# VectorE in program order through an attention stage, with the output bank emptied by ScalarE

## The chip, the core and the metric

The kernel runs on one core of one Trainium2 chip. The metric is the device time of one execution in microseconds. TensorE (PE in the profile) multiplies matrices and writes to the accumulation banks, VectorE (DVE) and ScalarE (ACT) read those banks, GpSimd (POOL) works on the on-chip memory alone, and SyncE (SP) issues the transfers.

## The reference

One layer of a hybrid encoder on 1024 frames of width 1024. Three mixers work on the same normalized input: latent attention (MLA, 8 heads), forgetting attention (FoX, 8 heads) and a state-space scan (SSM). Their outputs are merged with sigmoid gates, and a gated MLP follows. Cut to what matters here, it computes for each of the 16 attention heads, in blocks of 128 query rows:

```python
s = einsum('qd,kd->qk', q_blk, k) * scale          # scores of 128 rows
p = softmax(bias_mask(i, s), axis=-1)               # keys up to the row's own block
out = einsum('qk,kd->qd', p, v)
...
xBC = silu(causal_dwconv(xBC, conv_w, conv_b))      # depthwise convolution of the SSM input, 4 taps
g = sigmoid(u_gate + b_gate)                        # gates of the three mixers
```

## The kernel before

All matrices are float32. To keep the precision, each operand is split into a high and a low part, and a product is made of two or three passes over the parts.

**Stages.** Normalization and the projections come first, then the attention stage (about 435 to 980 us in the profile), the state-space stage (to about 1205 us), the merge of the branches, the output projection and the MLP. The change touches the attention stage, lines 870 to 1026.

**The fill.** Two projections have no hurry: the input of the convolution (12 blocks of 128 channels) and the gates (24 blocks). The generator `all_fill` (L777) makes them in 36 blocks of 48 matmuls of 128x512 (L794), and hands back control after every six, which it counts as 1.3 us. These matmuls fill TensorE wherever the attention and the state-space stage would leave it idle. Behind each convolution block `conv_done` (L748) sets a chain of later work: a scaling on GpSimd (L766), six multiply-adds on VectorE, the taps (L759), two tanh on ScalarE (L772), two products on VectorE (L763) and a store.

**How the order is made.** A model clock `clk` runs over the stage in the emitting program. `merge` (L821) takes pieces of several generators in turn, by the share of their planned time that is done, and advances the clock by each piece's planned cost. `later(us, fn)` (L704) puts an instruction into a queue with a due time; `run_until` emits those that are due. So there are two orders: the order in which the program emits, made of due times, and the order in which each engine gets its instructions. Under `tc.manual_schedule(engines={PE})` (L999) TensorE gets them as they are emitted. For the other engines a scheduler places them by its own simulation of the kernel.

**A row of scores** (`score_row`, L870). Row block i has i + 1 key blocks, in one chunk or, from the fifth on, in two. For each chunk two or three matmuls go into one of three banks `s` (L884), the mask is added by one more (L887), and VectorE takes the negative maximum (L889, due 0.1 us after the matmuls). With two chunks VectorE takes the smaller of both (L896, due at 0.8). ScalarE takes the exponential of each chunk (L899, due at 0.9), which frees the bank, and VectorE and GpSimd normalize the row (L904 to L906, due at 2.6).

**A unit of values** (`values`, L917). A unit is a pair of row blocks. The probabilities are transposed by TensorE into one of two banks `tp` (L952), ScalarE copies them as the high half (L957), VectorE subtracts for the low half (L958, due at 0.6), and the value matmuls (L924 to L932) add up in one half of the bank `o`, two pairs of key blocks later. Units take the two halves of this one bank in turn. At the unit's end `done` (L934) empties it: ScalarE copies partitions 64 to 127 (L937, due at 0.5), and VectorE adds partitions 0 to 63 to that copy (L940, due at 0.9); the result is stored to `att_d` (L941).

**The start and the end.** Ahead of the first head `merge([], 8.0)` (L1001) runs six pieces of fill alone. In the state-space stage the fill goes on with the shares of FILL_SSD (L986), until it is used up near the end of that stage; the last chunk's transposes (L1169) follow the norm at L1156 and L1161.

Of the kernel before, what the change touches and what calls it, by code (L numbers as in the profile page):

```python
# [11 lines left out]
F32 = mybir.dt.float32  # L12
# [3 lines left out]
AF = mybir.ActivationFunctionType  # L16
ALU = mybir.AluOpType
# [25 lines left out]
def block_kernel(ctx: ExitStack, tc: tile.TileContext, x, positions, norm_mix_g, w_in, b_gate,  # L43
# [5 lines left out]
    V, A, G, T, SY = nc.vector, nc.scalar, nc.gpsimd, nc.tensor, nc.sync  # L49
# [85 lines left out]
    def uid(s):  # L135
        cnt[0] += 1
        return f"{s}_{cnt[0]}"
# [566 lines left out]
    def later(us, fn):  # L704
        h = [clk[0] + us, uid(""), fn]
        queue.append(h)
        return h
# [106 lines left out]
    def advance(gen):  # L814
        c = next(gen, None)
        if c is not None:
            clk[0] += c
            run_until(clk[0])
        return c

    def merge(streams, fill_us):  # L821

        st = [[e[0], max(e[1], 0.01), 0.0, e[2] if len(e) > 2 else 0.0] for e in streams]
        owed[0] += fill_us
        if owed[0] > 0.65:
            st.append([fill, owed[0], 0.0, 0.0])
        while st:
            s_ = min(st, key=lambda e: e[3] + (1.0 - e[3]) * e[2] / e[1])
            if s_[0] is fill and s_[2] >= s_[1] - 0.65:
                owed[0] -= s_[2]  # L830
                st.remove(s_)
                continue
            c = advance(s_[0])
            if c is None:
                st.remove(s_)
            else:
                s_[2] += c
# [32 lines left out]
    def score_row(o, i, pn):  # L870
        mask = (mmla, mfox)[o.br]
        n = i + 1
        chunks = row_chunks(i)
        p_, _ = a_pm.get()
        nmx, _ = a_nmx.get()
        rs, rl = a_rs.get()
        pss = []
        qs = slice(i * P, i * P + P)
        for ci, (a, b) in enumerate(chunks):
            ps, pl = a_s.get()  # L880
            w = max(b - a, 256)
            last = ci == len(chunks) - 1
            for i_, (q_, k_) in enumerate(o.passes):
                T.matmul(ps[:, :w], q_[:, qs], k_[:, a:a + w], start=i_ == 0,  # L884
                         stop=not last and i_ == len(o.passes) - 1)
            if last:
                T.matmul(ps[:, b - a - P:b - a], identb, mask, start=False, stop=True)  # L887
            c = len(o.passes) * w / 2400
            later(c + 0.1, lambda ps=ps, ci=ci, a=a, b=b: V.reduce_max(  # L889
                nmx[:, ci:ci + 1], ps[:, :b - a], axis=AX, negate=True))  # L890
            pss.append((ps, pl))
            if not last:
                yield c
        two = len(chunks) == 2
        if two:
            later(c + 0.8, lambda: V.tensor_tensor(nmx[:, 2:3], nmx[:, 0:1], nmx[:, 1:2], op=ALU.min))  # L896
        nb = nmx[:, 2:3] if two else nmx[:, 0:1]
        for ci, (a, b) in enumerate(chunks):
            pss[ci][1][0] = later(c + 0.9 + 0.1 * ci, lambda ci=ci, a=a, b=b: A.activation(  # L899
                p_[:, a:b], pss[ci][0][:, :b - a], AF.Exp, bias=nb, accum_out=rs[:, ci:ci + 1]))  # L900

        def norm():
            if two:
                V.tensor_add(rs[:, 2:3], rs[:, 0:1], rs[:, 1:2])  # L904
            V.reciprocal(rs[:, 3:4], rs[:, 2:3] if two else rs[:, 0:1])  # L905
            G.tensor_scalar(p_[:, 0:n * P], p_[:, 0:n * P], rs[:, 3:4], 0.0, op0=ALU.mult, op1=ALU.add)  # L906

        rl[0] = later(c + 2.6, norm)
        pn.append((p_, rl))
        yield c + 0.05  # L910
# [6 lines left out]
    def values(o, jp, pn):  # L917

        po = o_acc[:, jp % 2, :]

        def pv(kp, th, tl):
            full = kp < jp
            k0, k1 = 2 * kp, 2 * kp + 1
            T.matmul(po, o.vv[:, k0, :], th[:, 0:256], start=kp == 0, stop=False)  # L924
            if full:
                T.matmul(po, o.vv[:, k1, :], th[:, 256:512], start=False, stop=False)
                T.matmul(po, o.vv[:, k1, :], tl[:, 256:512], start=False, stop=False)
            else:
                T.matmul(po[0:64, 128:256], o.vv[:, k1, 0:64], th[:, 256:384], start=False, stop=False)
                T.matmul(po[0:64, 128:256], o.vv[:, k1, 64:128], th[:, 256:384], start=False, stop=False)  # L930
                T.matmul(po[0:64, 128:256], o.vv[:, k1, 0:64], tl[:, 256:384], start=False, stop=False)
            T.matmul(po, o.vv[:, k0, :], tl[:, 0:256], start=False, stop=not full)  # L932

        def done():  # L934
            o1, l1 = a_o1.get()
            o2, l2 = a_o2.get()
            later(0.5, lambda: A.activation(o1, po[64:128, :], AF.Copy))  # L937

            def fin():
                V.tensor_add(o2, po[0:64, :], o1)  # L940
                SY.dma_start(att_d[o.br][o.h * 64:o.h * 64 + 64, jp * 256:jp * 256 + 256], o2)  # L941

            l1[0] = l2[0] = o_last[jp % 2] = later(0.9, fin)

        for _, rl in pn:
            force(rl[0])
        for kp in range(jp + 1):
            pt, pl = a_tp.get()
            off = 0
            for k in (2 * kp, 2 * kp + 1):  # L950
                for qi in ((0, 1) if k <= 2 * jp else (1,)):
                    T.transpose(pt[:, off:off + P], pn[qi][0][:, k * P:k * P + P], ident)  # L952
                    off += P
            th, _ = a_th.get()
            tl, _ = a_tl.get()
            c = 0.11 * off / P
            later(c + 0.05, lambda th=th, pt=pt, off=off: A.activation(th[:, :off], pt[:, :off], AF.Copy))  # L957
            pl[0] = later(c + 0.6, lambda th=th, tl=tl, pt=pt, off=off: V.tensor_sub(  # L958
                tl[:, :off], pt[:, :off], f32(th[:, :off])))
            pend.append((pv, kp, th, tl, pl, jp, done if kp == jp else None))  # L960
            yield c
            if len(pend) > PVLAG:
                run_pv()
                yield 0.44
# [3 lines left out]
    o_last = [None, None]  # L968
# [18 lines left out]
    with ExitStack() as pt__:  # L987
        atp = pt__.enter_context(TP("atp", 2))
        psp = pt__.enter_context(TP("psa", 1, space=PSUM))
        atp_lead = atp.tile([P, 64], F32, name="lead4", tag="lead4", bufs=1)  # L990
        a_pm = Ring(atp, [P, S], F32, "pm", 6)
        a_nmx, a_rs = (Ring(atp, [P, 4], F32, n, 4) for n in ("nmx", "rs"))
        a_th, a_tl = (Ring(atp, [P, 512], F32R, n, PVLAG + 2) for n in ("pth", "ptl"))
        a_o1 = Ring(atp, [64, 256], F32, "o1", 1)
        a_o2 = Ring(atp, [64, 256], F32, "o2", 2)
        a_s = Ring(psp, [P, 512], F32, "s", 3)
        a_tp = Ring(psp, [P, 512], F32, "tp", 2)
        o_acc = psp.tile([P, 2, 256], F32, name="o", tag="o")
        with tc.manual_schedule(engines={mybir.EngineType.PE}):  # L999
            names = [(br, h) for br in range(2) for h in range(8)]  # L1000
            merge([], 8.0)  # L1001
            units = [(n, jp) for n in range(16) for jp in range(4)]
            heads = {0: load_head(atp, *names[0])}
            load_values(atp, heads[0])
            done = []
            for n in range(len(units) + 2):
                st, share = [], 0.0
                if n < len(units):
                    hn_, jp = units[n]
                    if jp == 0 and hn_ + 1 < 16:  # L1010
                        heads[hn_ + 1] = load_head(atp, *names[hn_ + 1])
                    if jp == 3 and hn_ + 1 < 16:
                        load_values(atp, heads[hn_ + 1])
                    pn = []
                    done.append((heads[hn_], jp, pn))
                    share += cost_s(jp)
                    st.append((scores(heads[hn_], jp, pn), cost_s(jp, len(heads[hn_].passes))))
                if n >= 2:
                    share += cost_v(done[n - 2][1])
                    st.append((values(*done[n - 2]), cost_v(done[n - 2][1])))  # L1020
                merge(st, FILL_ATT * share)
            while pend:
                run_pv()
                clk[0] += 0.44
                run_until(clk[0])
            run_until(clk[0] + 3.0)
# [652 lines left out]
```

## Time and profile before

| | us |
|---|---|
| median of 3 runs | 2149.49 |
| lowest, highest | 2144.91, 2150.79 |
| the profiled execution | 2144.91 |
| its span, first to last instruction | 2143.0 |

The profile is of one execution. A row of the chain of waits reads: the engine and line that waited, the one that released it, the idle time in total, how often, and the longest. A row of a timeline reads: start, duration of all merged pieces, engine, line, operation, output and inputs, shape, count, and in brackets the engine's idle time before it and what ended it. A row of the busy time by stretch gives the busy microseconds of TensorE, its weight loads, VectorE, ScalarE and GpSimd, and then TensorE's granted clock (1.00 is full speed), the DMA share and GB/s. A row of the groups gives the busy time of a group, the mean duration in ns, and the idle time before it with what ended it.

### The profile page before, as it was taken

The numbers are of one execution on the slowest core, as the hardware profiler recorded it, in microseconds if no ns is written. First come the engines' busy times: TensorE is split into PE (matmuls) and PEld (weight loads), VectorE is DVE, ScalarE is ACT, GpSimd is POOL, SyncE is SP. The second block draws the span as 40 slices with busy tenths as digits, with TensorE's granted clock in tenths as the row PEclk, the third lists the DMA queues.
The fourth block names the chain that finished last, engine by engine and source line by source line (L and its number), as shares of the span: only waits on it lengthen the run. The fifth ranks groups of instructions, "written<-read, shape, count | busy, mean of one in ns | idle before, by whom it ended". The sixth has DMA issues, their size and how long they took to land.

```text
span 2143.0 us, 29100 instructions
## 1 busy us (share of the span) xinstructions
PE 2042.3 (95%) x10253; PEld 1689.7 (79%) x10253; DVE 1402.9 (65%) x2590; ACT 936.0 (44%) x1677; POOL 649.0 (30%) x620
## 2 busy tenths in 40 slices
PE   7999898999999999999999799999889999999999
PEld 6898677778888787787777688888668888887887
DVE  6687477346666566665888446557976677665665
ACT  5554222145555555554555213223444454545432
POOL 2453132212222222220000021002655544441855
PEclk9999999999999999999999899999899999999999
DMA  5167668654343544524342556441122222229765
GB/s 169 33 190 222 220 216 240 205 156 126 96 137 97 138 121 109 131 86 127 105 134 89 162 184 204 140 134 61 49 86 82 88 79 80 88 74 338 260 217 190
DMA packets 276649, 303.61 MB, mean 142 GB/s; under 512 B 19308, under 2 KB 209784, under 8 KB 276504
## 3 DMA queue, kind: packets, MB, share of 16 engines
q1 hardware_dynamic: 276504, 301.76, 46.0%
q8 instruction: 81, 1.33, 0.3%
q14 instruction: 64, 0.52, 0.1%
HBM read 209.03 MB, written 92.67 MB: 141 GB/s over the span
## 4 chain that ended last, share of the span: by engine, by line
PE 78%; DVE 7%; DMA 5%; POOL 3%; ACT 3%; issue 3%; SPq 0%; DVEq 0%; ACTq 0%; POOLq 0%
PE mm L794 16%; PE dn L1626 10%; PE ybr L167 8%; PE ua L1319 5%; PE fx L167 5%; PE uc L1319 5%; PE ud L1319 4%; PE wo L1364 4%; PE s L884 3%; PE tp L952 2%; PE ub L1319 2%; PE fxv L167 1%; DMA raw<-in_w_in_dram 1%; PE kv L167 1%; PE q L167 1%
## 5 line engine op out<-in xcount | busy, mean ns | idle before, releaser
L794 PE MATMUL mm<-hnh,wh 128*128 128x512 f32 x576 | 248.6, 432 | 0.0
L906 POOL TENSOR_SCALAR pm<-pm,rs 128x128 f32<-128x128 f32 (+7 forms) x128 | 110.2, 864 | 402.6 <-DVE rs L905 242.1
L794 PE MATMUL mm<-hnh,wl 128*128 128x512 f32 x576 | 226.9, 394 | 0.0
L794 PE MATMUL mm<-hnl,wh 128*128 128x512 f32 x576 | 226.1, 393 | 0.0
L1626 PE MATMUL dn<-dr,dr 128*128 128x512 f32 x592 | 182.1, 389 | 0.0
L899 ACT ACTIVATE pm<-s,nmx 128x128 f32<-128x128 f32 (+2 forms) x192 | 110.2, 579 | 97.6 <-DVE nmx L896 70.2
L958 DVE TENSOR_TENSOR ptl<-tp,pth 128x512 fp32r<-128x512 f32 (+1 forms) x160 | 100.2, 633 | 70.3 <-ACT pth L957 68.7
L889 DVE TENSOR_REDUCE nmx<-s 128x1 f32<-128x128 f32 (+2 forms) x192 | 105.5, 553 | 56.6 <-PE s L887 44.6
L884 PE MATMUL s<-qk,qk 96*128 96x384 f32 (+5 forms) x480 | 120.8, 356 | 13.0 <-ACT pm L899 11.4
L957 ACT ACTIVATE pth<-tp 128x512 fp32r<-128x512 f32 (+1 forms) x160 | 88.1, 554 | 99.5 <-PE tp L952 99.0
L1626 PEld LDWEIGHTS dn<-dr,dr 128*128 128x128 f32 x592 | 111.1, 188 | 22.9
L794 PEld LDWEIGHTS mm<-hnh,wl 128*128 128x128 f32 x576 | 108.4, 188 | 25.1
L794 PEld LDWEIGHTS mm<-hnl,wh 128*128 128x128 f32 x576 | 109.2, 190 | 17.1 <-issue 2.9
L794 PEld LDWEIGHTS mm<-hnh,wh 128*128 128x128 f32 x576 | 109.5, 190 | 16.6 <-issue 2.9
L1235 POOL TENSOR_TENSOR mg<-mg,gl 128x512 f32<-128x512 f32 x16 | 24.9, 1561 | 311.4 <-DVE gl L1232 311.3
L1626 PE MATMUL dn<-dr 128*128 128x512 f32 x296 | 115.2, 389 | 0.0
L167 PE MATMUL fx<-w5h,hnh 128*128 128x512 f32 x256 | 101.9, 402 | 7.9 <-ACT w5h L142 7.9
L143 DVE TENSOR_TENSOR dr<-dr,dr 128x1024 fp32r<-128x1024 f32 x52 | 75.3, 1449 | 49.9 <-ACT dr L142 41.8
L142 ACT ACTIVATE wh<-wr 128x1024 fp32r<-128x1024 f32 (+1 forms) x46 | 42.0, 913 | 147.6 <-PE ybr L167 69.6
L884 PEld LDWEIGHTS s<-qk,qk 96*128 96x128 f32 (+1 forms) x480 | 81.3, 192 | 26.4 <-ACT pm L899 16.2
L167 PE MATMUL ybr<-ah,wh 128*128 128x512 f32 x256 | 100.2, 396 | 1.6 <-ACT ah L142 1.6
L167 PE MATMUL fx<-w5h,hnl 128*128 128x512 f32 x256 | 101.4, 397 | 0.0
(457 smaller groups left out, 5855.7 us busy)
## 6 DMA issues: line engine op xcount, KB each, us to landing
dr<-act_d SPq DMA_DIRECT2D x99, 256.0 KB
wr<-in_ffn_w_up_dram SPq DMA_DIRECT2D x47, 512.0 KB
wr<-in_w_in_dram SPq DMA_DIRECT2D x36, 512.0 KB
g_d<-t SPq DMA_DIRECT2D x24, 512.0 KB
gl<-g_d SPq DMA_DIRECT2D x24, 512.0 KB
ws<-in_ffn_w_down_dram SPq DMA_DIRECT2D x22, 512.0 KB
wsum_d<-ws SPq DMA_DIRECT2D x22, 512.0 KB
act_d<-fa SPq DMA_DIRECT2D x22, 512.0 KB
```

The source lines that it names most:

```text
L143: return i, le.tensor_sub(l, src, f32(h))
L167: T.matmul(ps, a(k), b(k), start=(i == 0), stop=(i == n - 1))
L794: T.matmul(ps, a[:, k, :], b[half][:, k, :], start=(k == 0 and i == 0), stop=(k == NK - 1 and i == 2))
L884: T.matmul(ps[:, :w], q_[:, qs], k_[:, a:a + w], start=i_ == 0, stop=not last and i_ == len(o.passes) - 1)
L889: later(c + 0.1, lambda ps=ps, ci=ci, a=a, b=b: V.reduce_max(nmx[:, ci:ci + 1], ps[:, :b - a], axis=AX, negate=True))
L899: pss[ci][1][0] = later(c + 0.9 + 0.1 * ci, lambda ci=ci, a=a, b=b: A.activation(p_[:, a:b], pss[ci][0][:, :b - a], AF.Exp, bias=nb, accum ...
L906: G.tensor_scalar(p_[:, 0:n * P], p_[:, 0:n * P], rs[:, 3:4], 0.0, op0=ALU.mult, op1=ALU.add)
L957: later(c + 0.05, lambda th=th, pt=pt, off=off: A.activation(th[:, :off], pt[:, :off], AF.Copy))
L958: pl[0] = later(c + 0.6, lambda th=th, tl=tl, pt=pt, off=off: V.tensor_sub(tl[:, :off], pt[:, :off], f32(th[:, :off])))
L1319: T.matmul(ps, a, b, start=first and n == 0, stop=n == 11, skip_group_check=not first)
L1364: T.matmul(p, a, b, start=k == 0 and i == 0, stop=k == NK - 1 and i == 2)
L1626: T.matmul(ps[m], a[:, ts_], b[:, 512:], start=first_ and j == 0 and q == 0, stop=j == NFH - 1 and q == 2, skip_group_check=not first_)
```

## The change

- VectorE's instructions of the attention stage join the manual order: VectorE gets them in the order of their due times, as TensorE does.
- The smaller of both maxima is due at 0.11 instead of 0.8, right behind the second maximum.
- At a unit's end ScalarE copies both halves of the partitions (due at 0.3 and 0.31), so the addition takes both inputs from the on-chip memory; it is due at 2.2 instead of 0.9. The value matmuls that come next to the same half are put behind the second copy. The buffer `o1` of the first copy is doubled.
- The run of fill ahead of the first head is planned as 11.0 us instead of 8.0.

```diff
         if two:
-            later(c + 0.8, lambda: V.tensor_tensor(nmx[:, 2:3], nmx[:, 0:1], nmx[:, 1:2], op=ALU.min))
+            later(c + 0.11, lambda: V.tensor_tensor(nmx[:, 2:3], nmx[:, 0:1], nmx[:, 1:2], op=ALU.min))
...
-            later(0.5, lambda: A.activation(o1, po[64:128, :], AF.Copy))
+            later(0.3, lambda: A.activation(o1, po[64:128, :], AF.Copy))
+            o_last[jp % 2] = later(0.31, lambda: A.activation(o2, po[0:64, :], AF.Copy))
...
-                V.tensor_add(o2, po[0:64, :], o1)
+                V.tensor_add(o2, o2, o1)
...
-            l1[0] = l2[0] = o_last[jp % 2] = later(0.9, fin)
+            l1[0] = l2[0] = later(2.2, fin)
...
-        a_o1 = Ring(atp, [64, 256], F32, "o1", 1)
+        a_o1 = Ring(atp, [64, 256], F32, "o1", 2)
...
-        with tc.manual_schedule(engines={mybir.EngineType.PE}):
+        with tc.manual_schedule(engines={mybir.EngineType.PE, mybir.EngineType.DVE}):
...
-            merge([], 8.0)
+            merge([], 11.0)
```

## Prediction

> **What bounds the kernel now.** I read the page's first lines, then the busy time by stretch over the attention stage, then the chain of waits with TensorE alone as the waiting engine, and last the timelines around the longest of those waits.
>
> ```profile
> span 2143.0 us, 29100 instructions
> 435.00:960.00 525.00, 503.07 (x2947) 418.51 (x2948) 337.63 (x779) 281.61 (x689) 128.14 (x139) 0.99 0.44 117
> PE s L884 <- ACT pm L899: 11.4, 6, 3.1
> PE o L924 <- ACT o L937: 5.3, 9, 1.1
> PE o L924 <- DVE o L940: 3.1, 7, 0.8
> PE tp L952 <- POOL pm L906: 0.9, 1, 0.9
> PE s L884 <- DMA qk<-q_l: 0.8, 1, 0.8
> PE s L884 <- issue: 0.7, 1, 0.7
> ```
>
> The second row gives, after the window, the busy time of TensorE, its weight loads, VectorE, ScalarE and GpSimd. TensorE is busy 503 of 525 us: the stage is bound by it, and only about 22 us are open. The wait rows (total, number, longest) name nearly all of them, 22.2 us in 25 waits. So no edit here can win more than these waits and what they drag along; VectorE at 338 us and ScalarE at 282 us cost only where they come late.
>
> The biggest, scores waiting for the exponentials, has one cause, shown here at one of the bursts of taps (the depthwise convolution's multiply-adds, L759):
>
> ```profile
> 577.35 0.40 PE L794 MATMUL mm<-hnh,wh 128*128 128x512 f32 x1
> 580.36 1.75 POOL L766 TENSOR_SCALAR t<-t,pc_g 128x1024 f32<-128x1024 f32 x1 [2.24 <-ACT t L799]
> 582.34 1.41 DVE L759 SCALAR_TENSOR_TENSOR t<-t,pc_g,t 128x512 f32<-128x512 f32 x2
> 583.66 0.88 DVE L889 TENSOR_REDUCE nmx<-s 128x1 f32<-128x256 f32 x2
> 584.46 1.40 DVE L759 SCALAR_TENSOR_TENSOR t<-t,pc_g,t 128x512 f32<-128x512 f32 x2
> 585.78 0.15 DVE L896 TENSOR_TENSOR nmx<-nmx 128x1 f32<-128x1 f32 x1
> 586.03 0.58 ACT L899 ACTIVATE pm<-s,nmx 128x384 f32<-128x384 f32 x1 [4.87 <-DVE nmx L896]
> 586.75 0.79 PE L884 MATMUL s<-qk,qk 96*128 96x384 f32 x3 [1.92 <-ACT pm L899]
> 449.74 0.69 PE L884 MATMUL s<-qk,qk 96*128 96x384 f32 x1 [3.14 <-ACT pm L899]
> 722.43 0.62 PE L884 MATMUL s<-qk,qk 128*128 128x384 f32 x2 [2.37 <-ACT pm L899]
> 852.77 0.61 PE L884 MATMUL s<-qk,qk 128*128 128x384 f32 x2 [2.39 <-ACT pm L899]
> ```
>
> The code sets the taps 2.0 us apart, but they run back to back. Two stand ahead of the reductions, two more between the reductions (done at 584.54) and the tiny minimum at 585.78; the exponential waits for the minimum, the score bank for the exponential, and TensorE stands 1.92 us. The last three rows are the other bursts that reach TensorE: four in all, with 9.8 of the 11.4 us. Without taps the same place looks so:
>
> ```profile
> 549.68 0.42 DVE L889 TENSOR_REDUCE nmx<-s 128x1 f32<-128x256 f32 x1 [0.68 <-PE s L887]
> 550.34 0.58 ACT L899 ACTIVATE pm<-s,nmx 128x384 f32<-128x384 f32 x1 [1.93 <-DVE nmx L896]
> 551.92 0.51 PE L884 MATMUL s<-qk,qk 96*128 96x384 f32 x2
> ```
>
> The exponential ends at 550.92 and the bank is wanted at 551.92: the slack is 1.0 us. That is the number against which every delay on VectorE is weighed below.
>
> **The change part by part.** All sums are made against the profiled execution: 2144.91 us, of which the span is 2143.0. It is the fastest of the three runs; their median, 2149.49, lies 4.6 us above it, and I carry a difference over to the median unchanged.
>
> *VectorE in order, minimum behind the second reduction.* No instruction is added. Taps go back to one each 2.0 us, so between a reduction and its exponential stands at most one of them (0.70 us, half of the x2 pieces above, inside the slack of 1.0), and none between reduction and minimum. The six waits of 11.4 us should go. What is late next is VectorE's new head of line. The first tap is due 3.6 us after the start of the block's last six fill matmuls (577.35), that is at 580.95, but needs GpSimd's product, which ends at 582.11. Now everything due behind it waits about 1.15 us, then one tap. That is the usual case; the late one is this:
>
> ```profile
> 488.98 0.39 PE L794 MATMUL mm<-hnh,wh 128*128 128x512 f32 x1
> 494.07 1.20 POOL L766 TENSOR_SCALAR t<-t,pc_g 128x1024 f32<-128x1024 f32 x1
> DVE t L759 <- POOL t L766: 3.1, 4, 0.9
> L766 POOL TENSOR_SCALAR t<-t,pc_g 128x1024 f32<-128x1024 f32 x12 | 19.2, 1602 | 17.1 <-ACT t L799 17.1
> ```
>
> There GpSimd ends 6.29 us after the block's mark, 2.7 us behind the due time; four of the twelve convolutions were met by VectorE idle, and I take these four as the late ones. Queued behind the waiting tap are reductions, minima and the low halves of the probabilities (L958); for them wait ScalarE and, past the slack, TensorE. Bounds: nothing, if no tight place is met, and 8 x 1.15 + 4 x 2.7 = 20 us if every wait is passed on whole. I take one convolution in three as meeting a tight place, as four of the twelve do now, and there wait plus tap less slack: 8/3 x (1.15 + 0.70 - 1.0) + 4/3 x (2.7 + 0.70 - 1.0) = 5.5 us lost.
>
> *The first such wait drags the clock down.* It is the 3.14 us that end at 449.74, and around its end the granted clock (0.99 over the whole stage) reads:
>
> ```profile
> 448.75:455.57 6.82, 5.83 (x17) 4.64 (x18) 5.12 (x13) 3.89 (x11) 0.80 (x1) 0.50 0.12 48
> ```
>
> 6.82 us at 0.50, where full speed is 1.00, cost 6.82 x 0.5 = 3.4 us, which go with the wait. "TensorE: Matmul & The Clock Gate" of the Trainium skill, Part 1, puts the halving after at least one idle window of about 3.4 us; this trace halves after 3.1 us of idling, and not after the 1.9 us above, so by that rule the 3.4 us would stay only if a wait of such length stays at the start.
>
> *Output by two ScalarE copies.* Today one copy and one addition empty the bank, and the next unit's first value matmul waits for whichever the program put ahead of it:
>
> ```profile
> 496.84 0.41 DVE L940 TENSOR_TENSOR o<-o,o 64x256 f32<-64x256 f32 x1
> 771.08 0.38 ACT L937 ACTIVATE o<-o 64x256 f32<-64x256 f32 x1
> 771.52 0.39 PE L924 MATMUL o<-pth,vv 128*128 128x256 f32 x1 [1.12 <-ACT o L937]
> 770.44 0.62 ACT L772 ACTIVATE t<-t 128x512 f32<-128x512 f32 x1
> L937 ACT ACTIVATE o<-o 64x256 f32<-64x256 f32 x64 | 24.5, 382 | 38.8 <-PE o L932 35.9 <-issue 2.1
> ```
>
> The addition leaves PSUM's release path: the 3.1 us in seven waits go. In exchange ScalarE gets 64 x 0.382 = 24.4 us (282 becomes 306 of 525, still hidden as a total), and at the nine places where TensorE already waits for the first copy it now waits for the second too: 9 x 0.38 = 3.4 us more. Bounds: -5.3, if the earlier due time (0.3 instead of 0.5) takes the pair past the tanh that holds it up at 770.44, and +24.4 if each were exposed; I take the nine. The addition itself stays on VectorE at about its 0.41 us, and its store to att_d goes out 1.3 us later; it is read only after the stage, so I cost that at nothing.
>
> *Longer dense run.* 11.0 instead of 8.0 means two more pieces of six fill matmuls, about 12 x 0.23 = 2.7 us, ahead of the first scores:
>
> ```profile
> 434.28 0.39 PE L794 MATMUL mm<-hnh,wl 128*128 128x512 f32 x1
> 435.41 0.47 PE L884 MATMUL s<-qk,qk 96*128 96x256 f32 x2 [0.74 <-issue]
> 436.72 0.39 PE L884 MATMUL s<-qk,qk 96*128 96x256 f32 x1 [0.84 <-DMA qk<-q_l]
> ```
>
> They would run until 437.2, past the landing at 436.7, so both idle pieces, 1.6 us, are covered. The matmuls are moved, not added; their weights are loaded before the run starts. They are missing at the other end, where the fill runs dry in the state-space stage:
>
> ```profile
> 1192.55 0.40 PE L794 MATMUL mm<-hnh,wl 128*128 128x512 f32 x1
> 1199.39 1.06 ACT L1156 ACTIVATE yT<-y 128x1024 f32<-128x1024 f32 x1 [4.94 <-DMA ys_d<-yT]
> 1203.74 1.54 PE L1169 MATMUL stp<-ident,y 128*128 128x128 f32 x6 [10.36 <-ACT y L1161]
> ```
>
> That hole of 10.36 us is a store's landing and a chain behind it. The transposes that start it come after the last fill either way, so with TensorE's work before them unchanged it should open that much earlier and be as long: 0, at worst +2.7 if it grows by the matmuls taken away.
>
> **The sum:** -11.4 (scores) -3.4 (clock) -3.1 (addition) -1.6 (start) = -19.5; +5.5 (taps at the head of VectorE's line) +3.4 (second copy) = -10.6. 2144.9 becomes 2134.3, the median 2149.5 becomes 2138.9.
>
> **The rivals.**
>
> *The gain is given back in small pieces.* VectorE's own waits speak for it: it idles for ScalarE at L958, L904 and L905, and in order each such wait holds back the next reduction.
>
> ```profile
> DVE ptl L958 <- ACT pth L957: 68.7, 70, 3.2
> DVE rs L904 <- ACT pm L899: 38.2, 44, 1.5
> ```
>
> If another 48 tight reuses (three a head) lose 0.2 us each, 9.6 us, the sum is -1.0: 2148.5. Against it: the mean waits, 68.7/70 = 1.0 and 38.2/44 = 0.9 us, lie within the slack.
>
> *VectorE falls behind and stays behind (slower).* During a convolution taps take 0.70 us of every 2.0, after a first wait of 1.15 or 2.7. From the point where the ordered queue's backlog exceeds 1.0 us at a tight reuse, TensorE stands as it does behind a burst now; if all twelve convolutions reach that point, at the price of the cheapest burst, 12 x 1.92 = 23.0 us come in place of the 5.5: the sum is -19.5 + 23.0 + 3.4 = +6.9, 2156.4. "TensorE: Matmul & The Clock Gate" of the Trainium skill, Part 1, calls VectorE a strict first-in first-out engine, so on it nothing due can pass a tap that waits; the trace can't contradict this, as VectorE idled for GpSimd in front of a tap four times. For it also: 338 of 525 us busy before any added waiting. Against it: taps spread out leave 1.3 us in each 2.0, and today's bursts reach TensorE in only four cases.
>
> *The order hardly matters, only the start does.* Then the first wait, its clock and the start go (3.1 + 3.4 + 1.6), the second copy costs 3.4, and -4.7 remains: 2144.8, not to be told from no change.
>
> **How the numbers follow.** A measurement of this kernel can tell about 0.3%, 6.4 us. The forecast has 0.58; its own range is 2124 (all 19.5 gone and 5.3 of the copies' waits) to 2143. Given back, 0.12; start alone, 0.10; falls behind, 0.20. Faster by over 0.3%: 0.60, with 0.02 of the start-alone case; within: 0.21, with 0.01 of falling behind; slower: 0.19. The range of 8 in 10 reaches from 2124 to 2157, about the slower case's price.
>
> **What would show it.** Right: the row of scores waiting for exponentials falls below 4 us; taps stand singly about 2 us apart; the granted clock stays 1.00 at 448 to 456; no value matmul waits for L940; the score matmuls start near 437.2 without idling; ScalarE gains 64 copies of 0.38 us. Wrong: TensorE's idling in the stage stays above 20 us, with VectorE idle for GpSimd in front of L759 for about 1 us twelve times and score matmuls waiting at more than four heads; or the hole at L1169 grows by 2 us or more.

## The result, and the profile after

| | before | after |
|---|---|---|
| median of 4 executions, us | 2149.1 | 2128.88 |
| lowest to highest, us | 2144.91 to 2150.79 | 2127.69 to 2131.38 |
| the profiled execution, us | 2144.91 | 2131.38 |
| its span, us | 2143.0 | 2129.4 |

The ratio is 0.9917 with a 95% interval of 0.9903 to 0.9930: the change makes the kernel faster, by 20.2 us between the medians (their quotient alone is 0.9906, within the interval). The two profiled executions differ by only 13.5 us, because the profiled one of before is the fastest of its four and that of after the slowest of its four.

The page of after begins with the span and the busy time of the engines:

```profile
span 2129.4 us, 29118 instructions
PE 2036.1 (96%) x10238; PEld 1689.4 (79%) x10253; DVE 1405.0 (66%) x2590; ACT 954.9 (45%) x1741; POOL 653.1 (31%) x620
```

The busy time by stretch, over the attention stage and over the few microseconds that ran at half clock before (columns: TensorE, weight loads, VectorE, ScalarE, GpSimd, granted clock, DMA share, GB/s):

```profile
448.75:455.57 6.82, 6.45 (x34) 5.26 (x35) 5.05 (x14) 4.35 (x13) 2.04 (x3) 1.00 0.10 30
435.00:960.00 525.00, 512.33 (x3037) 431.12 (x3037) 345.97 (x788) 308.25 (x767) 134.95 (x143) 1.00 0.44 120
```

In the same 525 us TensorE is busy for 512 us instead of 503, and it runs 3037 matmuls instead of 2947. Its clock is 1.00 where it was 0.50. ScalarE's total rises from 282 to 308 us and stays hidden as a total.

The chain of waits, TensorE alone, from 430 to 985 us of after. These two rows are the whole answer; before there were six, with 22.2 us:

```profile
PE o L924 <- ACT o L938: 9.7, 14, 1.4
PE s L884 <- ACT pm L899: 3.0, 4, 1.2
```

The scores' waits fall from 11.4 to 3.0 us and the longest from 3.1 to 1.2. The waits for the addition are gone, and so are those at the start. What is left is for the most part a new row: value matmuls that wait for the second copy (L938, one line further down than in the kernel before, as is all behind it).

VectorE's timeline in after, around the place where before showed a burst of taps:

```profile
579.00 0.74 DVE L759 SCALAR_TENSOR_TENSOR t<-t,pc_g,t 128x512 f32<-128x512 f32 x1
579.66 0.55 DVE L889 TENSOR_REDUCE nmx<-s 128x1 f32<-128x384 f32 x1
581.72 0.74 DVE L759 SCALAR_TENSOR_TENSOR t<-t,pc_g,t 128x510 f32<-128x510 f32 x1
582.38 0.42 DVE L889 TENSOR_REDUCE nmx<-s 128x1 f32<-128x256 f32 x1
582.83 0.16 DVE L896 TENSOR_TENSOR nmx<-nmx 128x1 f32<-128x1 f32 x1
583.55 0.74 DVE L759 SCALAR_TENSOR_TENSOR t<-t,pc_g,t 128x512 f32<-128x512 f32 x1
```

The taps now stand singly, about two microseconds apart. Over the whole stage two of them follow each other directly in one place; before it was so in 24. The second reduction ends at 582.80 and the minimum starts at 582.83; before, two taps stood between them, from 584.54 to 585.78.

TensorE at the first head of after:

```profile
438.01 0.39 PE L794 MATMUL mm<-hnl,wh 128*128 128x512 f32 x1
438.24 0.52 PE L884 MATMUL s<-qk,qk 96*128 96x256 f32 x3
```

The fill hands over to the first scores without idling. To see what the stages are worth, I measure from the first matmul of the fill to the first matmul of the branch merge (`ybr`). The rows are those of the fill's line and of the timeline at the merge, first of before:

```profile
L794 PE MATMUL mm<-hnh,wh x576: 387/397/799, 426.3 to 1192.1; 128*128 128x512 f32 x192
1207.35 1.22 PE L167 MATMUL ybr<-ah,wh 128*128 128x512 f32 x2 [1.63 <-ACT ah L142]
```

and then of after:

```profile
L794 PE MATMUL mm<-hnh,wh x576: 387/397/799, 427.4 to 1178.1; 128*128 128x512 f32 x192
1190.90 1.97 PE L1170 MATMUL stp<-ident,y 128*128 128x128 f32 x8 [9.31 <-ACT y L1162]
1194.50 2.08 PE L167 MATMUL ybr<-ah,wh 128*128 128x512 f32 x4 [1.63 <-ACT ah L142]
```

That is 781.0 us before and 767.1 after: 13.9 us, the whole difference of the two profiled executions. Ahead of the fill and behind the merge they agree to about 1 us. The rest of the 20.2 us between the medians is in how the executions of one kernel differ. Only one execution of each was profiled, so where in the kernel the other executions of before spent theirs is open.

### The profile page after: what moved, and what is told of

It reads as the page before. It is cut to its first block, busy times and chain, and to the rows that moved or that the text cites. A ratio compares the mean times of both kernels' runs of the same rounds, so it can differ in the third digit from the quotient of the medians.

```text
span 2129.4 us, 29118 instructions
## 1 busy us (share of the span) xinstructions
PE 2036.1 (96%) x10238; PEld 1689.4 (79%) x10253; DVE 1405.0 (66%) x2590; ACT 954.9 (45%) x1741; POOL 653.1 (31%) x620
## 4 chain that ended last, share of the span: by engine, by line
PE 78%; DMA 8%; DVE 6%; ACT 3%; issue 2%; POOL 2%; SPq 1%; ACTq 0%; DVEq 0%; POOLq 0%
PE mm L794 16%; PE dn L1627 10%; PE ybr L167 8%; PE ua L1320 5%; PE fx L167 5%; PE ud L1320 4%; PE uc L1320 4%; PE wo L1365 4%; PE s L884 4%; DMA att_d<-o 3%; PE tp L953 2%; PE ub L1320 2%; PE cq L167 1%; PE q L167 1%; DMA fv_d<-fv 1%
## 5 line engine op out<-in xcount | busy, mean ns | idle before, releaser
L906 POOL TENSOR_SCALAR pm<-pm,rs 128x128 f32<-128x128 f32 (+7 forms) x128 | 119.0, 932 | 360.9 <-DVE rs L905 290.3
L959 DVE TENSOR_TENSOR ptl<-tp,pth 128x512 fp32r<-128x512 f32 (+1 forms) x160 | 101.2, 632 | 109.6 <-ACT pth L958 108.6
L899 ACT ACTIVATE pm<-s,nmx 128x128 f32<-128x128 f32 (+2 forms) x192 | 109.7, 575 | 59.7 <-DVE nmx L896 43.5
L167 PE MATMUL fx<-w5l,hnh 128*128 128x512 f32 x256 | 101.0, 396 | 0.0
```

The source lines that it names most:

```text
L167: T.matmul(ps, a(k), b(k), start=(i == 0), stop=(i == n - 1))
```

## The experiments

The theory was that the gain is the sum of the prediction's own terms: the ordered VectorE and the early minimum take the scores' waits and the half clock behind the first of them, the longer run takes the start, and the two copies give little or nothing. Against it stood that one part alone makes the gain (the order, the run or the copies), and that an edit costs time which another one covers. After the first experiments came the question of why the medians moved more than the profiles. The table collects what the sections below use. "Stage" is the time from first fill to `ybr` in the profile, "waits" the sum of the chain's rows for TensorE from 430 to 985 us, and "half clock" the time in that window at a granted clock of 0.50. Two things fall outside that window: the first scores of the order alone and of the first short run come before 430, with 0.5 and 0.9 us more of waits, and in after's second profile and with four buffers 3.4 us at half clock lie in the state-space stage (at 1098 and 1123 us). Each ratio is against executions of before on the same chip; the rows come from several chips, so ratios compare less well across rows than stages do.

| kernel | ratio to before | 95% interval | stage | waits | half clock |
|---|---|---|---|---|---|
| before | 1 | | 781.0 | 22.2 | 6.8 |
| after | 0.9917 | 0.9903 to 0.9930 | 767.1 | 12.7 | 0 |
| after, once more | 0.9905 | 0.9885 to 0.9925 | 765.9 | 10.5 | 0 |
| order alone | 0.9964 | 0.9952 to 0.9976 | 774.8 | 13.7 | 3.4 |
| after without the copies | 0.9893 | 0.9878 to 0.9908 | 761.0 | 7.2 | 0 |
| after with the short run | 0.9962 | 0.9947 to 0.9977 | 769.5 | 11.9 | 6.8 |
| the same once more, one execution | 0.9915 | | 771.1 | 13.7 | 10.2 |
| after with the late minimum | 0.9944 | 0.9930 to 0.9958 | 773.3 | 15.7 | 0 |
| run alone | 0.9977 | 0.9965 to 0.9989 | 778.2 | 18.0 | 0 |
| after without the order | 0.9963 | 0.9950 to 0.9977 | 779.3 | 18.5 | 6.8 |
| no copies, run of 14.0 | 0.9878 | 0.9855 to 0.9900 | 756.2 | 3.6 | 0 |
| after with four buffers o2 | 0.9888 | 0.9873 to 0.9903 | 763.7 | 8.8 | 0 |
| no copies, 14.0, free square | 0.9858 | 0.9842 to 0.9875 | 755.8 | 5.1 | 0 |
| after, ScalarE in order too | 0.9955 | 0.9937 to 0.9972 | 774.2 | 14.8 | 10.2 |

### The order alone

The edit, against before:

```diff
-        with tc.manual_schedule(engines={mybir.EngineType.PE}):
+        with tc.manual_schedule(engines={mybir.EngineType.PE, mybir.EngineType.DVE}):
```

> The kernel before with one edit: VectorE joins the manual order of the attention stage; the minimum stays at 0.8, the output's copy and addition and the run of 8.0 stay. Theory A (the order is what pays: it spreads the taps, so the waits of the scores for the exponentials fall from 11.4 to about 3 us and the 3.4 us of half clock go): 10 to 12 us below the kernel before, about 2138. Theory B (the longer run at the start pays): within 2 us of the kernel before. Theory C (the output's two copies pay): within 2 us of the kernel before. If the ordered VectorE needs the minimum moved too, the gain stays under 6 us.

Measured: 2135.72 against 2143.9 us, a ratio of 0.9964. TensorE's waits:

```profile
PE o L924 <- DVE o L940: 4.9, 9, 1.1
PE o L924 <- ACT o L937: 4.1, 9, 0.7
PE s L884 <- ACT pm L899: 3.5, 10, 0.6
```

The order by itself takes the long waits of the scores away (11.4 us with one of 3.1, now 3.5 us in ten small ones) and with them the half clock at 449. The value matmuls' waits stay where they were, 9.0 us against 8.4: the addition now takes its turn on VectorE. The start's waits remain, and here 3.4 us of half clock follow them, from about 431.5 on. So the order gives somewhat less than half of the gain: 8.2 us between the medians, short of the 10 to 12 of Theory A and more than the 6 that it should stay under if it needed the minimum moved too.

### The change without the copies

The edit, against after:

```diff
-            later(0.3, lambda: A.activation(o1, po[64:128, :], AF.Copy))
-            o_last[jp % 2] = later(0.31, lambda: A.activation(o2, po[0:64, :], AF.Copy))
+            later(0.5, lambda: A.activation(o1, po[64:128, :], AF.Copy))
...
-                V.tensor_add(o2, o2, o1)
+                V.tensor_add(o2, po[0:64, :], o1)
...
-            l1[0] = l2[0] = later(2.2, fin)
+            l1[0] = l2[0] = o_last[jp % 2] = later(0.9, fin)
...
-        a_o1 = Ring(atp, [64, 256], F32, "o1", 2)
+        a_o1 = Ring(atp, [64, 256], F32, "o1", 1)
```

> The kernel after with the old emptying of the output bank (one ScalarE copy at 0.5, the addition from the bank at 0.9, one buffer o1). Theory A: within 3 us of the kernel after, since its value matmuls wait 9.7 us for the copies where the kernel before waits 5.3 + 3.1; a little faster if the second copy is what makes up the difference. Theory C: 6 us or more slower than the kernel after, by value matmuls that wait for the addition at the head of a longer VectorE queue.

Measured: 2120.72 against 2143.9 us, 0.9893.

```profile
PE s L884 <- ACT pm L899: 2.6, 4, 0.9
PE o L924 <- ACT o L937: 2.4, 8, 1.0
PE o L924 <- DVE o L940: 2.2, 3, 1.1
```

With the old emptying the value matmuls wait 4.6 us; with the two copies they wait 9.7 and, in the second profile, 8.3. The stage is 5 to 6 us shorter without the copies (761.0 against 767.1 and 765.9). The medians of different chips can't settle 3 us, and the intervals of the ratios overlap, but the waits name the place. The copies take back part of what the other edits give.

### The short run, twice

The edit, against after:

```diff
-            merge([], 11.0)
+            merge([], 8.0)
```

> The kernel after with the run of fill in front at 8.0 again. Theory A: 1.5 us slower than the kernel after (the idle time of the first scores comes back), at most 3. Theory B: 8 us or more slower, with a wait of 3 us at the first burst and half the clock behind it.

> The kernel after with the run of 8.0 a second time, for its profile, since its median lay 9 us above the profiled execution. If the run in front is what differs between executions: the first scores wait 3 us or more for their loads. If it is another stage: the stretch from the first fill matmul to the merge takes 769 to 771 us again, and the time ahead of the first fill matmul differs from the 419.2 us of the first profile.

Measured: 2134.76 us (2125.71 to 2137.88) against 2143.9, 0.9962. The second time there was one execution, of 2128.4 us against 2146.68, which is 0.9915. With 11.0 the ratios were 0.9917 and 0.9905. So by the first six executions the three more microseconds of planned run are worth about 0.5%, some 10 us, and by the single one next to nothing; the size is not settled. The start itself is 1.3 us in the second profile, not the 3 us or more of the expectation, and the stage of 771.1 us is what it named for the other case. The second profile shows another part of the loss, first on TensorE:

```profile
818.54 0.58 PE L924 MATMUL o<-pth,vv 128*128 128x256 f32 x1 [3.42 <-ACT o L938]
```

then in the busy time by stretch:

```profile
805.00:817.00 12.00, 10.09 (x61) 8.03 (x59) 6.56 (x16) 7.25 (x20) 2.53 (x3) 1.00 0.92 248
817.20:824.00 6.80, 5.46 (x19) 4.58 (x20) 2.27 (x6) 2.36 (x7) 1.06 (x2) 0.50 0.53 120
854.80:858.20 3.40, 3.40 (x13) 2.70 (x12) 2.26 (x6) 1.16 (x3) 0.81 (x2) 0.50 0.58 216
```

and on ScalarE:

```profile
814.89 0.38 ACT L937 ACTIVATE o<-o 64x256 f32<-64x256 f32 x1 [0.29 <-PE o L932]
818.11 0.38 ACT L938 ACTIVATE o<-o 64x256 f32<-64x256 f32 x1 [2.84 <-DMA att_d<-o]
```

Up to 817 the transfer engines are full (0.92 of their time, 248 GB/s). A store to `att_d` lands late, the second copy waits 2.84 us for it, TensorE stands for 3.42 us, and 6.8 us run at half clock. The first profile has the same wait at 818.33 (2.94 us) with 3.4 us at half clock behind it, and another 3.4 us at half clock at the start, from 430 on. So the short run exposes waits whose price is the clock behind them, and one of them belongs to the copies. In the profiles this makes 2.4 to 5.2 us of stage time, and not the 10 us of the medians: the profiled execution of the first six is the fastest of them. The others were not profiled, but each execution's mean granted clock was taken: 0.985 for the profiled one and 0.981 for the slowest. Estimated from these, the clock takes (1 - 0.981) x 2137.9 = 40.6 us of the one and 31.9 of the other, 8.7 of the 12.2 us between them. The second slowest, at 0.984, has only 2.3 of its 10.6 us from there. The clock is one part of what they lost, and the rest is open.

### The late minimum

The edit, against after:

```diff
-            later(c + 0.11, lambda: V.tensor_tensor(nmx[:, 2:3], nmx[:, 0:1], nmx[:, 1:2], op=ALU.min))
+            later(c + 0.8, lambda: V.tensor_tensor(nmx[:, 2:3], nmx[:, 0:1], nmx[:, 1:2], op=ALU.min))
```

> The kernel after with the minimum due at 0.8 again. Theory A: 0 to 3 us slower, since at most one tap or one low half comes between the reduction and the minimum. If the minimum's place is the part that pays, 6 us or more slower, with the waits of the scores for the exponentials above 8 us.

Measured: 2131.87 against 2143.9 us, 0.9944.

```profile
PE o L924 <- ACT o L938: 9.1, 12, 1.6
PE s L884 <- ACT pm L899: 6.6, 14, 1.2
```

The early place is worth 6 to 8 us by the ratios (0.9944 against 0.9917 and 0.9905) and 6.2 to 7.4 us by the stage. I had put it at 0 to 3. On an ordered VectorE, what is due between 0.11 and 0.8 us stands ahead of the minimum whether its own input is there or not. The scores' waits rise from 2.2 and 3.0 us to 6.6, in fourteen places instead of four. These 4 us are shown, short of the 8 us of waits that the second forecast named; the other 2 to 3 us of the stage are in no row that I found.

### The change once more

Nothing is edited: the same kernel beside other executions of the kernel before.

> The kernel after once more, so that it stands beside the others on one chip. Both theories: about 0.992 of the kernel before, its runs within 4 us of each other.

Measured: 2125.86 us (2122.43 to 2130.26) against 2146.05, 0.9905.

```profile
PE o L924 <- ACT o L938: 8.3, 11, 1.4
PE s L884 <- ACT pm L899: 2.2, 4, 0.9
```

The gain of 20 us repeats, and so do both rows. The stage takes 765.9 us, 1.2 less than in the first profile. The five executions spread over 7.8 us, twice what I expected.

### The longer run alone

The edit, against before:

```diff
-            merge([], 8.0)
+            merge([], 11.0)
```

> The kernel before with the longer run of fill alone (11.0). The kernel after with the short run spread over 12 us and its median lay far above its profiled execution. Theory A2 (the longer run pays in the executions in which the first head's loads land late): 5 to 9 us below the kernel before, the runs within 5 us of each other, while the scores' waits for the exponentials stay near 11 us in the profile. Rival B2 (the run only moves the convolutions against the heads): within 3 us of the kernel before or off by whatever the shifted bursts cost, with as wide a spread as the kernel before.

Measured: 2141.2 us (2137.11 to 2145.66) against 2146.05, 0.9977.

```profile
PE s L884 <- ACT pm L899: 10.7, 8, 2.5
PE o L924 <- DVE o L940: 3.0, 4, 1.0
```

The start's waits are gone, and with the longest score wait at 2.5 us there is no half clock anywhere in the stage; the other score waits are as large as before. The stage is 2.8 us shorter, and the medians differ by 4.9, at the lower end of the 5 to 9 of Theory A2. I had thought that the run might bring the executions within 5 us of each other; the twelve here spread over 8.5 us, so it does not (the twenty of before beside them spread over 12.7).

### The change without the order

The edit, against after:

```diff
-        with tc.manual_schedule(engines={mybir.EngineType.PE, mybir.EngineType.DVE}):
+        with tc.manual_schedule(engines={mybir.EngineType.PE}):
```

> The kernel after without VectorE in the manual order: the minimum at 0.11, the two copies and the longer run stay. Theory A: 8 to 14 us slower than the kernel after, with the bursts of taps back and the scores' waits for the exponentials above 8 us. If the order pays nothing by itself: within 3 us of the kernel after.

Measured: 2139.73 against 2146.05 us, 0.9963.

```profile
PE s L884 <- ACT pm L899: 10.1, 8, 2.5
PE o L924 <- ACT o L938: 6.2, 9, 1.4
```

An earlier due time of the minimum shows no effect on the scores' waits as long as the scheduler places VectorE's instructions: they are 10.1 us, against 11.4 before and 10.7 with the longer run alone. With two of these waits, of 2.10 us up to 449.36 and of 2.52 us up to 892.61, come 3.4 us of half clock each. Without the order the kernel loses 12 to 13 us of stage time. By the stage the order carries the gain: the other edits without it are worth 1.7 us, the order without them 6.2, and all together 13.9 to 15.1. The minimum's place pays only together with the order. In the medians it is less clear: without the order the kernel still gains 0.37%, as much as the order alone does (0.36%), and the two add up to most of the 0.83 to 0.95%.

### No copies and a still longer run

The edit, against the change without the copies:

```diff
-            merge([], 11.0)
+            merge([], 14.0)
```

> The kernel after without the two copies, and with the run in front at 14.0 instead of 11.0 (18 more fill matmuls, about 4.1 us). Theory A2: the loads have landed by then already, so 0 to 2 us around the kernel without copies at 11.0, which was 0.9893 of the kernel before. Rival: each piece moved to the front is taken from the end of the state-space stage, so 2 to 4 us slower, by a longer hole at the last transposes.

Measured: 2120.43 us (2112.14 to 2127.22) against 2146.05, 0.9878.

```profile
PE o L924 <- DVE o L940: 1.7, 4, 0.9
PE o L924 <- ACT o L937: 1.1, 1, 1.1
PE s L884 <- ACT pm L899: 0.6, 2, 0.3
```

The waits fall to 3.6 us and the stage by another 4.8 us, to 756.2, which neither forecast had. The rival was right about the end: from the last fill matmul to `ybr` it is 18.4 us here and 16.2 in the kernel without copies at 11.0. The waits saved ahead of it outweigh that. In the medians the step from 0.9893 to 0.9878 lies within the intervals. These executions spread over 15 us, more than any other kernel's here.

### Four buffers for the output

The edit, against after:

```diff
-        a_o2 = Ring(atp, [64, 256], F32, "o2", 2)
+        a_o2 = Ring(atp, [64, 256], F32, "o2", 4)
```

This tests what the second copy waits for. In after, ScalarE's own waits hold this row:

```profile
ACT o L938 <- DMA att_d<-o: 10.8, 7, 2.9
```

One of the seven, put together from the timelines of four engines (VectorE, SyncE's queue, ScalarE, TensorE):

```profile
854.94 0.41 DVE L941 TENSOR_TENSOR o<-o,o 64x256 f32<-64x256 f32 x1
855.38 0.53 SPq L856 DMA_DIRECT2D qk<-fq_l  x1
856.47 0.47 SPq L942 DMA_DIRECT2D att_d<-o  x1
865.15 0.38 ACT L937 ACTIVATE o<-o 64x256 f32<-64x256 f32 x1 [0.92 <-PE o L932]
868.42 0.38 ACT L938 ACTIVATE o<-o 64x256 f32<-64x256 f32 x1 [2.90 <-DMA att_d<-o]
868.85 0.39 PE L924 MATMUL o<-pth,vv 128*128 128x256 f32 x1 [1.37 <-ACT o L938]
```

The addition at 854.94 and the store issued at 856.47 belong to two units earlier, and so to the same of the two buffers `o2`. That store stands in the queue behind a head's loads, and the semaphore that lets the second copy go comes at 868.40, 11.9 us after its issue. The first copy has its own buffer and writes at once. The trace links the seven waits to stores that are issued among or behind a head's loads (at 699, 731, 759, 763, 825, 856 and 889 us) and let their buffer go 8 to 12 us later. Before, `o2` was first written by the addition, planned at 0.9 us, and its store followed at once. Now it is written at 0.31 us, and the store that must be done first is issued behind an addition due at 2.2. The buffer is held longer at the one end and wanted sooner at the other.

> The kernel after with four buffers o2 instead of two. Theory D (the two copies cost because the second one now writes o2 early, while the store of two units before, issued later than it was, still reads it): the 10.8 us in which ScalarE waits for the store vanish, the value matmuls' waits for the second copy fall from 9.7 to about 6 us, 2 to 5 us faster than the kernel after. Rival E (it is the second copy's own 0.38 us at every tight unit end): waits stay at 8 to 10 us, within 2 us of the kernel after.

Measured: 2121.99 against 2146.68 us, 0.9888.

```profile
PE o L924 <- ACT o L938: 6.6, 9, 1.4
PE s L884 <- ACT pm L899: 2.2, 4, 0.9
```

The store's row is gone from ScalarE's waits, and the value matmuls wait 6.6 us instead of 9.7 and 8.3. The stage is 2.2 to 3.4 us shorter. The intervals of the ratios overlap with those of after (0.9903 to 0.9930 and 0.9885 to 0.9925), so it is the rows that show this. What remains, 2.0 us between 6.6 and the 4.6 of the old emptying, is within the copy's own time at nine waits (9 x 0.38 = 3.4 us).

### The last square in a buffer of its own

The edit, against no copies, 14.0:

```diff
-            A.activation(o.yT.rearrange("p j s -> p (j s)"), yf, AF.Square, accum_out=ss)
+            sqt = o.yT.rearrange("p j s -> p (j s)")
+            if c + 1 == NT:
+                sqt = pool.tile([P, 16, 64], F32, name=uid("xd"), tag="xd", bufs=1).rearrange("p h d -> p (h d)")
+            A.activation(sqt, yf, AF.Square, accum_out=ss)
```

The hole ahead of the last transposes starts with a wait for a store: the square is written into `yT`, which is still being stored. Only the buffer of a value that nobody reads changes.

> The kernel without the two copies and with the run at 14.0, and with the last chunk's square written to another buffer, so that it needn't wait for the store of the chunk before. Only the buffer of a value that nobody reads changes. If that store is what holds the last transposes: their hole of 9 us falls by 3 to 5, and the time by as much, to about 0.986 of the kernel before. If the chain of the norm is: within 1 us.

Measured: 2115.63 us (2114.43 to 2119.64) against 2146.68, 0.9858, the fastest version here. TensorE's wait at the hole was, with the square in `yT`:

```profile
PE stp L1169 <- ACT y L1161: 9.3, 2, 8.6
```

and is now:

```profile
PE stp L1172 <- ACT y L1164: 7.3, 2, 6.6
```

The hole closes by 2.0 us, which is neither the 3 to 5 that I expected nor within 1; that the ratio came out at the expected 0.986 is luck. The stretch at half clock that begins in the hole falls from 13.7 to 10.2 us. The stage is only 0.4 us shorter, since this profile's value matmuls happen to wait 1.5 us longer; the intervals of the two ratios overlap, so 2.0 us is what the hole shows and the medians can't confirm it.

### ScalarE in order as well

The edit, against after:

```diff
-        with tc.manual_schedule(engines={mybir.EngineType.PE, mybir.EngineType.DVE}):
+        with tc.manual_schedule(engines={mybir.EngineType.PE, mybir.EngineType.DVE, mybir.EngineType.Activation}):
```

> The kernel after with ScalarE in the manual order as well. If the scheduler's order on ScalarE is what delays the output's copies: the value matmuls' waits fall below 5 us, some 4 us faster. If an ordered ScalarE waits at its head (low halves' sources, tanh behind taps): 10 us or more slower than the kernel after.

Measured: 2136.88 against 2146.68 us, 0.9955.

```profile
PE o L924 <- ACT o L938: 13.5, 12, 3.0
PE s L884 <- ACT pm L899: 1.3, 4, 0.4
```

That is 8 to 11 us more than after by the ratios, near the rival's 10, and 7 to 8 us by the stage. ScalarE's own waits show why:

```profile
ACT pm L899 <- DVE nmx L896: 75.4, 44, 3.2
```

In after that row is 43.5 us. An exponential that waits for its minimum now holds back the copies due behind it, and the value matmuls pay: three of their waits (2.29, 3.02 and 2.74 us) come with 3.4 us of half clock each. An order by due times helps an engine whose due times fit; as these waits read, ScalarE's do not.

## Why the prediction was right, and where it was not

The forecast of a gain held, and by its own mechanism: the order, the minimum and the run act where they were said to. The two copies take the addition's waits away, but cost more than they save. Point by point, against the profile:

- **The scores, -11.4.** Measured -8.4 (11.4 to 3.0). The bursts are gone and the taps stand singly. That the order does it is shown by the pair of runs: alone it leaves 3.5 us, and without it 10.1 remain.
- **The clock, -3.4.** Right. The stretch from 448.75 to 455.57 runs at 1.00. Of the Trainium skill's "TensorE: Matmul & The Clock Gate", Part 1, the prediction took that an idle window of about 3.4 us is needed. These runs disagree: waits of 2.00, 2.10 and 2.29 us came with half clock, while waits of 2.37 and 2.39 us in before did not.
- **The addition's waits, -3.1.** Right: the row is gone.
- **The start, -1.6.** Right in size (1.5 us in the two rows), the first scores 1 us later than said. What the step lacked is the clock behind these waits: in two of the profiles with a run of 8.0, 3.4 us of half clock follow the start.
- **VectorE's head of line, +5.5.** This is the term that was mis-sized. I had each of the twelve convolutions hold VectorE for 1.15 or 2.7 us. VectorE's own waits for GpSimd in after read:

```profile
DVE ptl L959 <- ACT pth L958: 108.6, 94, 3.6
DVE rs L904 <- ACT pm L899: 7.3, 10, 1.8
DVE t L759 <- POOL t L766: 2.1, 4, 0.9
```

  It is 2.1 us in four waits. The last row shows that, and the first two show what fills the time instead: much of VectorE's line ahead of a tap waits for ScalarE anyway. It did so before as well, in other places: the waits at the low halves rise from 68.7 to 108.6 us, while those at L904 fall from 38.2 to 7.3, and this row of before falls to 0.7:

```profile
DVE rs L905 <- ACT pm L899: 15.8, 27, 1.2
```

  A tap in an ordered line is late together with its line, and GpSimd is done by then; that is how I read these rows, and no run tests it. The most that this can have cost TensorE is the 3.0 us of score waits that are left.
- **The second copy, +3.4.** The row says +4.4 (5.3 to 9.7), near the number, but the mechanism failed in part. The step "its store to att_d goes out 1.3 us later; it is read only after the stage, so I cost that at nothing" looked at the reader of the store and not at the buffer that it reads from. Four buffers take that wait away: 10.8 us on ScalarE, 2 to 3 us on TensorE. Together with the addition's -3.1 I had the new emptying at +0.3; against the old one under the same order it loses 5 to 6 us of stage. There the addition's waits are 2.2 us and the first copy's 2.4, where before had 3.1 and 5.3. I compared the copies with the emptying in the kernel before, whose waits the other three edits together bring down (the order alone leaves 9.0).
- **The tail, 0 to +2.7.** From the last of the fill's rows above to the merge it is 15.2 us before and 16.4 after, so 1.2 us came back here, while the wait in the hole fell from 10.36 to 9.31. Two shorter waits of transposes (1.4 us up to 1105.5 and 1.3 up to 1131.8) and some small ones are new in the state-space stage. All of TensorE's waits from the end of the attention stage to `ybr` rise from 12.0 to 14.9 us, with the longer run alone as well, so the +2.7 that the prediction put as the worst case is nearer than its 0. From within the hole on the clock is at 0.50 in both kernels (17.1 us from 1196.26 before, 13.7 us from 1186.05 after), which no term of the prediction holds.
- **The minimum.** I gave it no price of its own. It is worth some 6 us on top of the order.

The measured terms add up to -8.4 - 3.4 - 3.1 - 1.5 + 4.4 = -12.0, with -0.9 for a wait of the transposes on GpSimd that is gone: -12.9 us up to the end of the attention stage. The 2.9 us of waits that came back behind it leave -10.0, so 3.9 of the 13.9 us of the stage are in no wait and no stretch of half clock, and where TensorE saved them is open. The prediction had -10.6 for the profiled execution and 2134.3 us, against 2131.38. The scores and VectorE's head of line together were put at -5.9 and came to -8.4, which is nearly all of that difference.

The step that missed the median is the last one: "I carry a difference over to the median unchanged". The profiles differ by 13.5 us, the medians by 20.2 and, in the second comparison, by 20.2 again (2146.05 to 2125.86). The profiled execution of before was its fastest. A kernel whose waits lie near the point at which the clock halves can lose more in one execution than in another; the short run shows that kind of loss in two places (at the start and at 818). For the executions of before the mean granted clock speaks for it: of the twenty in the second comparison the four at 0.981 or less take 2149.8 us on average, the eight at 0.983 or more 2143.6. Which waits those were is not shown.

Of the rivals, "VectorE falls behind" fell with the 2.1 us. "The order hardly matters" fell with the run without it, by the stage. "Given back in small pieces" named a row that did grow (VectorE's waits at the low halves, by 40 us), but the waits at L904 and L905 fell by 46, and it costs little: all the score waits in the stage are 3.0 us.

## What to carry to other kernels

When an engine that is not the bound places its work in bursts, look at what waits for the smallest instruction behind the burst; an explicit order can be worth more than any faster instruction, and a due time, like that of the minimum here, may matter only once the order is explicit. When a write moves forward or a store moves back, ask of every buffer who still reads it, the store included, and not only who reads the result. And cost a combined change against the kernel in which the other edits are already made: half of the waits that the two copies were meant for had gone with the other edits.

## What the runs showed of the hardware

The clock halves after shorter waits than I had taken. TensorE's waits at the half clock were 2.10 and 2.52 us (the change without the order), 2.29, 2.74 and 3.02 us (ScalarE in order), 2.94 us (the short run) and 2.00 us (its second profile), each with about 3.4 us at 0.50; 3.14 us (before) and 3.42 us (the short run's second profile) had 6.8 us. Waits of 2.37 and 2.39 us (before) and of 2.07 and 2.52 us (the longer run alone) left the clock at 1.00. At the start of the order alone and of the first short run, 3.4 us at half clock came with two idle pieces of 0.5 to 1.2 us, while before and the short run's second profile had two such pieces without it. So the length of a wait doesn't decide alone.

Where the wait falls does much of the rest. Within one execution the changes of the clock lie on a grid of 3.41 us (before: 448.75, 455.57 and 1196.26, which is 2 and 219 steps from the first). Count TensorE's busy share from one point of this grid to the next. In the attention stages of all fourteen profiles the clock halves eleven times; in nine of them TensorE was busy for 20 to 50% of the 3.41 us that end there, in the other two, both at the start, for 53 and 56%. Of the some 2260 other stretches at full clock only one lies below 50% (before, 718.40 to 721.81, 49%) and three more below 56%. The two waits of 2.52 us show it: without the order TensorE is busy 1.71 of the 3.41 us from 890.91 on and the clock halves; with the longer run alone a point of the grid falls into the wait, TensorE is busy 2.28 us from 888.41 on and 2.02 us from 891.82 on, and the clock stays. The rule is read off these traces and was not tested by a run of its own.

The Trainium skill, "TensorE: Matmul & The Clock Gate", Part 1, tells of a free-running window of activity of about 3.4 us: the lengths of 3.4 and 6.8 us and the grid agree with that, but a whole window of idling was not needed. The stretch of 6.8 us in the short run's second profile begins at 817.24, before TensorE starts again at 818.54.

In after, the 64 KB stores of seven units, issued among or behind a head's loads, held their source buffer for 7.9 to 12.1 us.

The time at which the first fill matmul starts, which no edit touches, lies between 419.2 and 429.4 us over the profiles. That spread of 10 us is as large as most of the effects here, so differences below it are read from the stage and from the waits, not from the end of a single execution.
